# A hybrid attention and SSD decoder layer: norm blocks fetched up to four ahead and multiplied 26 steps later, one convolution at a time, second readers emitted later

## The chip, the cores and the metric

The kernel runs on one core of a Trainium2 chip. The metric is the device time of one execution in microseconds (us), and of several executions the median. Engines go by the profile's names: PE is TensorE (PEld its weight loads), DVE is VectorE, ACT is ScalarE, POOL is GpSimd, SP is SyncE, which issues the DMAs here; SPq is its queue of them.

## The reference

One decoder layer over 512 prompt tokens and 8 x 8 sampled tokens, 576 in all, with 2048 features:

```python
h = rmsnorm(x, norm_pre)
u = jnp.einsum('btd,de->bte', h, w_in)
q, k, v, g_a, z, xbc, dt = jnp.split(u, SPLIT_POINTS, axis=-1)
o_a = swa_prompt(q, k, v, attn_sink)
attn_out = rmsnorm(o_a * jax.nn.silu(g_a), attn_norm)
xbc_c = jax.nn.silu(causal_conv(xpad, conv_w, conv_b))
y, h_new = ssd(xs, dt, A, Bm, Cm, h0, chunk)
yz = (y + d_skip * xs) * jax.nn.silu(z)
ssm_out = rmsnorm(yz, ssm_norm)
mix = jnp.concatenate([attn_out, ssm_out], axis=-1)
out = jnp.einsum('bte,ed->btd', mix, w_out)
return x + rmsnorm(out, norm_post), new_k, new_v, new_conv, h_new
```

(Cut: shapes, masks and the sampled tokens' branch are left out.) `ssm_out` is normed in four groups of 512 features, `attn_out` over all 2048. The caches, the convolution's tails and the states are outputs too. All is fp32.

## The kernel before

*The matmuls.* Features lie on the 128 partitions, the 576 tokens along the free axis in two halves of 288. fp32 accuracy comes from three passes: weight tile and activation are each split into a rounded half and a rest, and `mm3` issues three matmuls of 128x128 by 128x288 (lines 348 to 350): high by high, high by rest, rest by high. A unit of weights, 128x512, is loaded into one of nine `raw` buffers (line 309), rounded into `w[:, 0]` by ACT (line 329), and its rest is taken by DVE (line 332) into `w[:, 1]`; there are four `w` buffers, so a unit is split up to three ahead. In most of the input product a unit serves eight calls of `mm3`. Column tiles come singly or, later, in pairs, which save one product in eight and need sums of weight units on POOL (line 269). The input product's columns come in the order of four head groups of the state part (B, C and four x tiles each, with the z gates between), then keys, values, queries and gates of attention; the output product runs in two passes, first over the state half of `mix`, then over the attention half.

*The order of work.* Nothing is scheduled by the compiler: instructions stand on each engine in the order in which the program emits them. The main program emits the matmuls and calls `sch.tick()` once before each `mm3`: a step. Everything else, some two dozen kinds of side task, is a Python generator on the class `Schedule`: it emits a few instructions and says by `yield n` that it goes on n steps later. `yield from wait(...)` asks again at each step. If the main program itself lacks a buffer it ticks on without a matmul, so that side work is emitted with no matmul between. An engine executes its instructions strictly in that order and stands where one has to wait; so do SP's transfers.

*The parts that the change touches.* `renorm` (line 1129) finishes the norm of a head group (four blocks of 128 features) or of attention (sixteen). The blocks lie in DRAM, in `m_d`; their factors, one a token, are stored to `r_d` (lines 838 and 839, in `finish`) and read back over all partitions by `factors` (line 845) 8 steps later. Then, 10 steps on, one block after the other: load (line 1135), 8 steps, multiply by the factors and gamma on DVE (line 1137), a step, store to `m_d` (line 1139), a step. 32 blocks in all.

`conv_task` (line 1157) takes one 128-feature tile of B, C or x: first tap on ACT (line 1163), three taps on DVE (line 1166), tanh on ACT (line 1168), gate on DVE (lines 1171, 1175). It holds two of four `scratch` buffers, U and y; the main program takes one for each new tile (line 1190). The first two tiles, B and C of group 0, have been kept raw and start together (`conv_raw`). There are 24 tiles, and a single column tile takes 32 steps.

`qb_task` (line 937) is one pair of attention heads and 256 queries: scores, softmax, transposes into the bank `pt` (line 1003), copies of `pt` to `pT[1]` by ACT (line 1010) and, masked, to `pT[0]` by DVE (line 1012 or 1014), 9 steps, value matmuls (line 1024). `sample` (line 1338) updates the sampled tokens' states: a matmul into the bank `pS` (line 1382), 2 steps, an addition on DVE (line 1385). `dt_task` (line 728) is a chain of some 20 small DVE instructions (lines 747 to 770) on the step sizes, once, early on.

Of the kernel before, what the change touches and what calls it, by code (L numbers as in the profile page):

```python
# [172 lines left out]
def wait(cond):  # L173
    while not cond():
        yield 1
# [3 lines left out]
def kern(ctx: ExitStack, tc: tile.TileContext, a: dict, o: dict):  # L179
    nc = tc.nc  # L180
    V, S, G, PE = nc.vector, nc.scalar, nc.gpsimd, nc.tensor
    dma = nc.sync.dma_start
# [17 lines left out]
    sch = Schedule()  # L200
# [7 lines left out]
    slots = Slots(sch, [f"S{i}" for i in range(NBIG)], make)  # L208
# [40 lines left out]
    m_d = [dr.tile([P, T], F32, name=f"m_d{j}", tag=f"m_d{j}") for j in range(32)]  # L249
# [592 lines left out]
    def factors(k):  # L842

        t = yield from slots.get()
        dma(t[:, :T], bass.AP(tensor=r_d.tensor, offset=r_d.offset + k * T, ap=[[0, P], [1, T]]))
        return t
# [90 lines left out]
    def qb_task(st, jj, m, u):  # L937
# [70 lines left out]
        pT4 = [t[:, :512].rearrange("p (f q k) -> p f q k", f=2, q=2) for t in pT]  # L1008

        S.copy(pT[1][:, :512], pt)  # L1010
        if f:
            V.tensor_tensor(pT4[0][:, :, 1], ptv[:, :, 1], stri.unsqueeze(1).broadcast_to([P, 2, P]), ALU.mult)
        else:
            V.tensor_tensor(pT[0][:, :512].rearrange("p (e k) -> p e k", e=4), pt.rearrange("p (e k) -> p e k", e=4),
                            stri.unsqueeze(1).broadcast_to([P, 4, P]), ALU.mult)
        banks.put(pt)
        yield 9
        for q in range(2):
            qb = 2 * m + q
            w0 = 0 if qb else 1  # L1020
# [108 lines left out]
    def renorm(k0, row, gamma):  # L1129

        Rt = yield from factors(row)
        yield 10
        for k in k0:
            t = yield from slots.get()
            dma(t, m_d[k])
            yield 8
            V.scalar_tensor_tensor(t, t, gamma[:, k % 16:k % 16 + 1], Rt, op0=ALU.mult, op1=ALU.mult)
            yield 1
            dma(m_d[k], t)
            yield 1  # L1140
            slots.put(t)
            ready["m", k] = True
        slots.put(Rt)
# [6 lines left out]
    class Group:  # L1150
        def __init__(self, g):
# [2 lines left out]
            self.done = set()  # L1154
            self.M, self.mid = {}, 0

    def conv_task(grp, name, box, k):
        U = box[0]
        Us = U[:, 515:603].rearrange("p (b w) -> p b w", w=11)
        G.tensor_copy(tails[:, k, 0], U[:, 512:515])  # L1160
        G.tensor_copy(tails[:, k, 1:9], Us[:, :, 8:11])
        y = yield from scratch.get()
        S.activation(y[:, :600], U[:, 0:600], AF.Identity, scale=cw[:, k, 0:1], bias=cw[:, k, 4:5])  # L1163
        yield 3
        for w in range(1, 4):
            V.scalar_tensor_tensor(y[:, :600], U[:, w:w + 600], cw[:, k, w:w + 1], y[:, :600], op0=ALU.mult, op1=ALU.add)  # L1166
            yield 2
        S.activation(U[:, :600], y[:, :600], AF.Tanh)
        yield 3
        dst = yield from slots.get()  # L1170
        V.scalar_tensor_tensor(dst[:, :TP], U[:, :TP], 1.0, y[:, :TP], op0=ALU.add, op1=ALU.mult)

        def smp(t):
            return t[:, 515:603].rearrange("p (b w) -> p b w", w=11)[:, :, 0:8]
        V.scalar_tensor_tensor(dst[:, TP:T].rearrange("p (b w) -> p b w", w=8), smp(U), 1.0, smp(y), op0=ALU.add, op1=ALU.mult)
        scratch.put(U, y)
        if name[0] == "C":
            if grp.g > 1:
                yield from wait(lambda: len(groups[grp.g - 2].done) == 5)
            G.tensor_copy(Cs[grp.g % 2][:, 0:TS], dst[:, TP:T])  # L1180
        yield 2
        grp.bc[name[0] if name[0] != "x" else name[2]] = dst
# [155 lines left out]
    def sample(grp, n, cs, C, Bt, xes, sms, E):  # L1338
# [34 lines left out]
        def seq(b, h0):  # L1373
            w = b // 4
            yield from wait(lambda: b < 2 or b - 2 in issued)
            Bs = BR[:, 2 * P + P * (b % 2):3 * P + P * (b % 2)]
            S.activation(Bs[:96], Bw[w][:96].bitcast(F32), AF.Copy, scale=bsel4[:96, b % 4:b % 4 + 1])
            hv = h0[:, :512].rearrange("p (h d) -> p h d", h=8)
            G.tensor_tensor(hv, hv, dch[:, 4 + b, h8].unsqueeze(2).broadcast_to([P, 8, 64]), ALU.mult)  # L1379
            yield 13  # L1380
            pS = yield from banks.get()
            PE.matmul(pS, Bs[:96], Xs[w][:96], start=True, stop=True)
            issued.add(b)
            yield 2
            V.tensor_tensor(h0[:, :512], h0[:, :512], pS, ALU.add)
            banks.put(pS)
            yield 2
            dma(o["ss"][g, :, b], h0[:, :512])
            smalls.put(h0)
            fin.append(b)  # L1390
# [70 lines left out]
    for entry[0] in range(len(PROGRAM)):  # L1461
# [17 lines left out]
        else:  # L1479
            f, t = conv_block(groups[g], name)  # L1480
# [44 lines left out]
    def attn_end():  # L1525
        yield from wait(lambda: attn_done[0] == 18)
        yield from sumA.finish(4 * D, 0)
        yield 8
        yield from renorm(range(16), 0, gam[0])
# [279 lines left out]
```

## Time and profile before

| | |
|---|---|
| median of 3 runs | 1655.22 us (1653.7 to 1661.37) |
| the profiled execution: its own time, and its span | 1653.8 us, 1652.0 us |
| granted TensorE clock, mean over the span | 0.981 |
| busy PE, DVE, ACT, POOL | 1598.8, 1095.8, 771.1, 389.4 us |
| moved by DMA | 222.98 MB, 135 GB/s over the span |

The span is the profiler's, from the first to the last instruction; the time has 1.8 us more around it. Busy time of PE counts a matmul from its start to its modelled end, and matmuls overlap, so holes are seen as missing busy time in short stretches, not as a share of the whole. A wait is put down to the instruction that stands first on its engine; all behind it waits with it.

### The profile page before, as it was taken

How to read it: one execution, taken by the hardware profiler on the slowest of the kernel's cores; microseconds unless marked ns; L12 is line 12 of the kernel's file. 1: busy time of each engine (PE TensorE's matmuls, PEld its weight loads, DVE VectorE, ACT ScalarE, POOL GpSimd, SP SyncE). 2: the span in 40 equal slices, each digit the busy share in tenths (PEclk: the TensorE clock that was granted, in tenths of full speed). 3: DMA queues.
4: the chain of work that ended last, by engine and by line, in shares of the span. 5: the costliest groups of instructions: out<-in, count | busy, mean ns of one | idle time of the engine just before them, and what ended most of it. 6: DMA issues, size and time to landing. Idle time of an engine off the chain costs nothing.

```text
span 1652.0 us, 31869 instructions
## 1 busy us (share of the span) xinstructions
PE 1598.8 (97%) x12158; PEld 1542.6 (93%) x12158; DVE 1095.8 (66%) x2185; ACT 771.1 (47%) x1849; POOL 389.4 (24%) x420
## 2 busy tenths in 40 slices
PE   8999999999999999999999999999999999999995
PEld 8899999999989998998999999999899999999995
DVE  7656755775667567476778868777686455655556
ACT  6433433444434445364655636656573322544440
POOL 3201222221312220342223213222111211023323
PEclk9999999999999999999999999999999999999997
DMA  6324356546565648446314322323461356723235
GB/s 238 89 74 110 90 180 187 146 163 188 142 154 160 186 131 279 132 134 135 103 58 126 87 75 75 97 71 109 132 201 46 96 153 216 271 86 103 91 100 186
DMA packets 157977, 222.98 MB, mean 135 GB/s; under 512 B 32160, under 2 KB 66080, under 8 KB 157792
## 3 DMA queue, kind: packets, MB, share of 16 engines
q1 hardware_dynamic: 157824, 220.95, 44.5%
q8 instruction: 95, 1.56, 0.4%
q14 instruction: 58, 0.48, 0.1%
HBM read 182.26 MB, written 40.60 MB: 135 GB/s over the span
## 4 chain that ended last, share of the span: by engine, by line
PE 80%; DVE 8%; DMA 6%; ACT 2%; issue 2%; SPq 1%; POOL 0%; DVEq 0%; ACTq 0%; POOLq 0%
PE bank L348 23%; PE bank L350 23%; PE bank L349 22%; DMA s<-m_d 4%; PE bank L1024 2%; DVE w L332 1%; DMA r_d<-t 1%; DVE u L1166 1%; PE bank L1286 1%; PE bank L1003 1%; DMA s<-z_d 1%; PE bank L954 1%; PE bank L955 1%; PE bank L1298 1%; DVE s L1667 1%
## 5 line engine op out<-in xcount | busy, mean ns | idle before, releaser
L348 PE MATMUL bank<-x,w 128*128 128x288 f32 x3288 | 999.9, 304 | 6.4 <-DVE eT L420 2.6
L350 PE MATMUL bank<-x,w 128*128 128x288 f32 x3288 | 983.4, 299 | 17.2 <-DVE w L332 17.2
L349 PE MATMUL bank<-x,w 128*128 128x288 f32 x3288 | 980.6, 298 | 1.8 <-DVE x L542 1.8
L348 PEld LDWEIGHTS bank<-x,w 128*128 128x128 f32 x3288 | 625.7, 190 | 26.5 <-issue 15.1
L350 PEld LDWEIGHTS bank<-x,w 128*128 128x128 f32 x3288 | 626.8, 191 | 19.2 <-DVE w L332 19.2
L349 PEld LDWEIGHTS bank<-x,w 128*128 128x128 f32 x3288 | 625.8, 190 | 7.2 <-issue 3.8
L332 DVE TENSOR_TENSOR w<-raw,w 128x512 fp32r<-128x512 f32 x476 | 386.7, 818 | 130.4 <-ACT w L329 120.5
L329 ACT CAST w<-raw 128x512 fp32r<-128x512 f32 x476 | 289.4, 615 | 270.5 <-PE bank L349 226.0
L269 POOL TENSOR_TENSOR raw<-raw,raw 128x512 f32<-128x512 f32 x52 | 78.0, 1499 | 190.9 <-issue 163.3
L1166 DVE SCALAR_TENSOR_TENSOR u<-u,c_convwb,u 128x600 f32<-128x600 f32 x72 | 67.4, 940 | 24.0 <-ACT u L1163 22.9
L269 POOL TENSOR_TENSOR raw<-sum,raw 128x512 f32<-128x512 f32 x26 | 33.8, 1300 | 182.2 <-DVE w L332 171.2
L991 ACT ACTIVATE m<-m,t 128x128 f32<-128x128 f32 x128 | 49.9, 391 | 38.7 <-DVE t L986 38.7
L1236 ACT ACTIVATE m<-m,a_tok 128x128 f32<-128x128 f32 (+1 forms) x160 | 53.3, 381 | 19.3 <-DMA m<-aT_d 19.3
L998 ACT ACTIVATE m<-m,t 128x128 f32<-128x128 f32 x128 | 41.0, 392 | 45.5 <-DVE t L995 45.4
L542 DVE TENSOR_TENSOR x<-s,x 128x288 fp32r<-128x288 f32 x112 | 48.4, 479 | 18.9 <-ACT x L537 18.6
L830 POOL TENSOR_TENSOR s<-s,s 128x512 f32<-128x512 f32 (+2 forms) x42 | 46.0, 1096 | 56.2 <-ACT s L828 55.6
L1379 POOL TENSOR_TENSOR m<-m,dch 128x512 f32<-128x512 f32 x32 | 38.0, 1216 | 89.4 <-PE bank L1401 47.4
L1631 POOL TENSOR_TENSOR s<-s,s 128x288 f32<-128x288 f32 x28 | 23.0, 825 | 149.1 <-ACT s L1628 149.1
L269 POOL TENSOR_TENSOR sum<-raw,raw 128x512 f32<-128x512 f32 x26 | 35.5, 1366 | 94.1 <-DMA raw<-in_win_dram 56.1
L1272 POOL TENSOR_TENSOR m<-m,de 128x512 f32<-128x512 f32 (+1 forms) x20 | 25.3, 1264 | 112.9 <-DVE m L1265 96.7
L1163 ACT ACTIVATE u<-u,c_convwb 128x600 f32<-128x600 f32 x24 | 21.2, 889 | 65.5 <-DVE u L443 61.7
L1434 POOL TENSOR_TENSOR s<-s,s 128x576 f32<-128x576 f32 x16 | 24.8, 1552 | 98.2 <-DMA s<-z_d 88.2
(254 smaller groups left out, 1766.8 us busy)
## 6 DMA issues: line engine op xcount, KB each, us to landing
raw<-in_win_dram SPq DMA_DIRECT2D x304, 256.0 KB
raw<-in_wout_dram SPq DMA_DIRECT2D x128, 256.0 KB
s<-m_d SPq DMA_DIRECT2D x80, 288.0 KB
m_d<-s SPq DMA_DIRECT2D x48, 288.0 KB
s<-in_xT_dram SPq DMA_DIRECT2D x40, 288.0 KB
m<-aT_d SPq DMA_DIRECT2D x32, 256.0 KB
m<-in_h0T_dram SPq DMA_DIRECT2D x32, 256.0 KB
out_ss_dram<-m SPq DMA_DIRECT2D x32, 256.0 KB
```

Of the source, the lines that this page charges most:

```text
L269: G.tensor_tensor(dst, x, y, op)
L329: S.copy(w[:, 0], x)
L332: V.tensor_tensor(w[:, 1], x, w[:, 0].bitcast(F32), ALU.subtract)
L348: PE.matmul(out, w[:, 0, c], x[:, 0], start=start, stop=False, skip_group_check=True)
L349: PE.matmul(out, w[:, 0, c], x[:, 1], start=False, stop=False, skip_group_check=True)
L350: PE.matmul(out, w[:, 1, c], x[:, 0], start=False, stop=stop, skip_group_check=True)
L542: V.tensor_tensor(t[:, 1], src, t[:, 0].bitcast(F32), ALU.subtract)
L830: G.tensor_tensor(self.acc[:, c0:c0 + n], self.acc[:, c0:c0 + n], sq[:, :n], ALU.add)
L991: S.activation(p4[:, e], p4[:, e], AF.Exp, bias=nm[:, e:e + 1], scale=0.125, accum_out=den[:, e:e + 1])
L998: S.activation(p4[:, e], p4[:, e], AF.Copy, scale=den[:, e:e + 1])
L1166: V.scalar_tensor_tensor(y[:, :600], U[:, w:w + 600], cw[:, k, w:w + 1], y[:, :600], op0=ALU.mult, op1=ALU.add)
L1236: S.activation(Mv[q][:n, h, :n], Mv[q][:n, h, :n], AF.Relu, bias=a_tok[:n, c, k:k + 1], scale=-1.0)
```

## The change

Three edits, all in the order of emission. In `renorm` the loads are a task of their own, 8 steps apart, with up to four blocks loaded and not yet multiplied, as long as more than five buffers are free; a block is multiplied 26 steps after its load, and its store stands 3 steps behind. The load task starts 5 steps after the factors' reload (4, and one until it runs). In `conv_task` a flag lets one convolution's taps run at a time, and the waits between its instructions are longer. In `qb_task` DVE's copy of `pt` comes 4 steps after ACT's, and the value matmuls 8 after that; in `sample` the addition comes 5 steps after its matmul. No instruction that computes is added or taken away.

```diff
@@ -1008,13 +1008,14 @@
         pT4 = [t[:, :512].rearrange("p (f q k) -> p f q k", f=2, q=2) for t in pT]
 
         S.copy(pT[1][:, :512], pt)
+        yield 4
         if f:
             V.tensor_tensor(pT4[0][:, :, 1], ptv[:, :, 1], stri.unsqueeze(1).broadcast_to([P, 2, P]), ALU.mult)
         else:
             V.tensor_tensor(pT[0][:, :512].rearrange("p (e k) -> p e k", e=4), pt.rearrange("p (e k) -> p e k", e=4),
                             stri.unsqueeze(1).broadcast_to([P, 4, P]), ALU.mult)
         banks.put(pt)
-        yield 9
+        yield 8
         for q in range(2):
             qb = 2 * m + q
             w0 = 0 if qb else 1
@@ -1129,13 +1130,23 @@
     def renorm(k0, row, gamma):
 
         Rt = yield from factors(row)
-        yield 10
-        for k in k0:
-            t = yield from slots.get()
-            dma(t, m_d[k])
-            yield 8
+        ahead, k0 = [], list(k0)
+
+        def load():
+            for k in k0:
+                yield from wait(lambda: len(ahead) < 4 and len(slots.free) > 5)
+                t = yield from slots.get()
+                dma(t, m_d[k])
+                ahead.append((k, t, sch.t + 26))
+                yield 8
+
+        yield 4
+        sch.spawn(load())
+        for _ in k0:
+            yield from wait(lambda: ahead and ahead[0][2] <= sch.t)
+            k, t, _ = ahead.pop(0)
             V.scalar_tensor_tensor(t, t, gamma[:, k % 16:k % 16 + 1], Rt, op0=ALU.mult, op1=ALU.mult)
-            yield 1
+            yield 3
             dma(m_d[k], t)
             yield 1
             slots.put(t)
@@ -1154,19 +1165,24 @@
             self.done = set()
             self.M, self.mid = {}, 0
 
+    conv_busy = [False]
+
     def conv_task(grp, name, box, k):
         U = box[0]
         Us = U[:, 515:603].rearrange("p (b w) -> p b w", w=11)
         G.tensor_copy(tails[:, k, 0], U[:, 512:515])
         G.tensor_copy(tails[:, k, 1:9], Us[:, :, 8:11])
+        yield from wait(lambda: not conv_busy[0])
+        conv_busy[0] = True
         y = yield from scratch.get()
         S.activation(y[:, :600], U[:, 0:600], AF.Identity, scale=cw[:, k, 0:1], bias=cw[:, k, 4:5])
-        yield 3
+        yield 6
         for w in range(1, 4):
             V.scalar_tensor_tensor(y[:, :600], U[:, w:w + 600], cw[:, k, w:w + 1], y[:, :600], op0=ALU.mult, op1=ALU.add)
-            yield 2
+            yield 3
+        conv_busy[0] = False
         S.activation(U[:, :600], y[:, :600], AF.Tanh)
-        yield 3
+        yield 6
         dst = yield from slots.get()
         V.scalar_tensor_tensor(dst[:, :TP], U[:, :TP], 1.0, y[:, :TP], op0=ALU.add, op1=ALU.mult)
 
@@ -1381,7 +1397,7 @@
             pS = yield from banks.get()
             PE.matmul(pS, Bs[:96], Xs[w][:96], start=True, stop=True)
             issued.add(b)
-            yield 2
+            yield 5
             V.tensor_tensor(h0[:, :512], h0[:, :512], pS, ALU.add)
             banks.put(pS)
             yield 2
```

How the order changes, in three places. First DVE at the first convolutions: `u` are their buffers; line 1166 before, 1181 now, is a tap, 1171 and 1175, now 1187 and 1191, the gate; 443 evicts a matmul's bank, and 332 takes a weight unit's rest. Before:

```order
L1166 SCALAR_TENSOR_TENSOR u_846<-u_832,c_convwb,u_846 128x600
L1171 SCALAR_TENSOR_TENSOR s_861<-u_827,u_842 128x512
L1175 SCALAR_TENSOR_TENSOR s_861<-u_827,u_842 128x64
L1171 SCALAR_TENSOR_TENSOR s_864<-u_832,u_846 128x512
L1175 SCALAR_TENSOR_TENSOR s_864<-u_832,u_846 128x64
L443 TENSOR_TENSOR u_868<-bank_71,R 128x288
L443 TENSOR_TENSOR u_868<-bank_72,R 128x224
L443 TENSOR_TENSOR u_868<-bank_72,R 128x8x8
L1166 SCALAR_TENSOR_TENSOR u_876<-u_868,c_convwb,u_876 128x600 x3
L332 TENSOR_TENSOR w_98<-raw_91,w_98 128x512
```

Now:

```order
L1181 SCALAR_TENSOR_TENSOR u_842<-u_827,c_convwb,u_842 128x600
L332 TENSOR_TENSOR w_98<-raw_91,w_98 128x512
L1181 SCALAR_TENSOR_TENSOR u_842<-u_827,c_convwb,u_842 128x600 x2
L332 TENSOR_TENSOR w_95<-raw_92,w_95 128x512
L1187 SCALAR_TENSOR_TENSOR s_929<-u_827,u_842 128x512
L1191 SCALAR_TENSOR_TENSOR s_929<-u_827,u_842 128x64
L332 TENSOR_TENSOR w_96<-raw_93,w_96 128x512
L1181 SCALAR_TENSOR_TENSOR u_932<-u_832,c_convwb,u_932 128x600 x2
L332 TENSOR_TENSOR w_97<-raw_85,w_97 128x512
L443 TENSOR_TENSOR u_977<-bank_70,R 128x288
```

Before, six taps (the last is shown), the gates, three evictions and three further taps stood in one piece ahead of the next weight split. Now weight splits stand among the first tile's and the second's taps, and the third tile's follow later, among the dt chain (lines 747 to 770):

```order
L747 MEMSET s_1056 128x32
L749 TENSOR_TENSOR s_1056<-bank_68,s_689 128x128
L749 TENSOR_TENSOR s_1056<-bank_68,s_689 64x32
L752 SCALAR_TENSOR_TENSOR s_1056<-s_1056 128x160
L1181 SCALAR_TENSOR_TENSOR u_1021<-u_850,c_convwb,u_1021 128x600
L757 TENSOR_SCALAR s_1056<-s_1056 128x160
L758 RECIPROCAL s_1056<-s_1056 128x160
L759 TENSOR_TENSOR s_1056<-s_1056 128x160
L760 TENSOR_TENSOR s_1057<-s_1056 128x160
L761 TENSOR_SCALAR s_1057<-s_1057 128x160
L1181 SCALAR_TENSOR_TENSOR u_1021<-u_850,c_convwb,u_1021 128x600
L332 TENSOR_TENSOR w_96<-raw_88,w_96 128x512
```

Nine instructions of that chain and two taps stand here between one weight split and the next.

Then DVE in group 1, where a multiply (line 1137, now 1148) stands near the scan (lines 1318 to 1330, now 1334 to 1346). Before:

```order
L1166 SCALAR_TENSOR_TENSOR u_4928<-u_4920,c_convwb,u_4928 128x600
L1137 SCALAR_TENSOR_TENSOR s_4914<-s_4914,c_gssm,s_4879 128x576
L1318 TENSOR_TENSOR m_4730<-bank_68,m_4730 128x512
L1320 TENSOR_TENSOR m_4730<-m_4730,bank_71 128x512
L1330 SCALAR_TENSOR_TENSOR s_3542<-s_3542,c_dskip,m_4730 128x128
L1330 SCALAR_TENSOR_TENSOR s_3718<-s_3718,c_dskip,m_4730 128x128
L1330 SCALAR_TENSOR_TENSOR s_3892<-s_3892,c_dskip,m_4730 128x128
L1330 SCALAR_TENSOR_TENSOR s_4026<-s_4026,c_dskip,m_4730 128x128
L1166 SCALAR_TENSOR_TENSOR u_4928<-u_4920,c_convwb,u_4928 128x600
L332 TENSOR_TENSOR w_98<-raw_92,w_98 128x512
```

Now:

```order
L1334 TENSOR_TENSOR m_4801<-bank_67,m_4801 128x512
L1336 TENSOR_TENSOR m_4801<-m_4801,bank_68 128x512
L1346 SCALAR_TENSOR_TENSOR s_3566<-s_3566,c_dskip,m_4801 128x128
L1346 SCALAR_TENSOR_TENSOR s_3740<-s_3740,c_dskip,m_4801 128x128
L1346 SCALAR_TENSOR_TENSOR s_3919<-s_3919,c_dskip,m_4801 128x128
L1346 SCALAR_TENSOR_TENSOR s_4055<-s_4055,c_dskip,m_4801 128x128
L1148 SCALAR_TENSOR_TENSOR s_4906<-s_4906,c_gssm,s_4881 128x576
L332 TENSOR_TENSOR w_96<-raw_85,w_96 128x512
```

The multiply of block 20 now stands behind the scan's instructions and directly ahead of a weight split; before, it stood ahead of the scan, with the next weight split behind that.

Last SP in the norm of attention: line 1135, now 1139, loads a block, 1139, now 1150, stores it, 309 loads weights. Before:

```order
L1139 DMA m_d_108<-s_14882 128x576
L1135 DMA s_14923<-m_d_109 128x576
L309 DMA raw_93<-in_wout_dram 128x512
L309 DMA raw_85<-in_wout_dram 128x512
L1139 DMA m_d_109<-s_14923 128x576
L1135 DMA s_14964<-m_d_110 128x576
L1139 DMA m_d_110<-s_14964 128x576
```

Now:

```order
L1139 DMA s_14899<-m_d_111 128x576
L1150 DMA m_d_108<-s_14798 128x576
L309 DMA raw_93<-in_wout_dram 128x512
L309 DMA raw_85<-in_wout_dram 128x512
L1139 DMA s_14934<-m_d_112 128x576
L1150 DMA m_d_109<-s_14832 128x576
L1139 DMA s_14967<-m_d_113 128x576
L1150 DMA m_d_110<-s_14862 128x576
```

Before, a block's store stood directly ahead of the next block's load, and the load of block 10 (`m_d_110`) directly ahead of its own store. Now the loads of the three blocks after it stand between a block's load and its store.

## Rows read from the trace of the kernel before

**Rows 1.** The page: busy us (share of the span) xinstructions of each engine.
```profile
PE 1598.8 (97%) x12158; PEld 1542.6 (93%) x12158; DVE 1095.8 (66%) x2185; ACT 771.1 (47%) x1849; POOL 389.4 (24%) x420
```

**Rows 2.** Stretches: us, busy PE, PEld, DVE, ACT, POOL, clock, DMA share, GB/s.
```profile
60.00:85.00 25.00, 21.26 (x138) 20.43 (x137) 18.78 (x38) 9.77 (x15) 7.87 (x15) 0.86 0.20 55
85.00:110.00 25.00, 24.04 (x159) 22.61 (x158) 15.18 (x38) 6.80 (x13) 0.58 (x4) 0.86 0.36 91
...
460.00:480.00 20.00, 16.12 (x111) 15.88 (x110) 11.62 (x20) 6.02 (x15) 2.79 (x4) 0.91 0.70 187
630.00:650.00 20.00, 17.21 (x119) 16.75 (x119) 18.80 (x42) 12.92 (x32) 1.32 (x1) 0.83 0.82 263
755.00:775.00 20.00, 16.31 (x109) 15.62 (x109) 10.36 (x20) 8.75 (x26) 4.09 (x4) 0.83 0.66 210
800.00:1100.00 300.00, 299.79 (x2399) 288.81 (x2400) 232.38 (x492) 171.06 (x486) 79.98 (x73) 1.00 0.29 87
1215.00:1225.00 10.00, 8.15 (x65) 7.29 (x64) 7.04 (x20) 6.93 (x24) 0.00 (x0) 1.00 0.45 143
1335.00:1395.00 60.00, 54.78 (x384) 53.94 (x383) 33.37 (x50) 15.89 (x28) 12.11 (x8) 0.94 0.63 202
1400.00:1425.00 25.00, 25.00 (x190) 25.00 (x189) 16.59 (x35) 11.54 (x28) 0.00 (x0) 1.00 0.90 310
1450.00:1550.00 100.00, 100.00 (x753) 100.00 (x753) 55.48 (x86) 41.83 (x85) 32.30 (x30) 1.00 0.28 88
```

**Rows 3.** Waits, whole span: who waited for whom, total us, times, longest.
```profile
DVE s L1137 <- DMA s<-m_d: 71.4, 27, 7.5
...
DVE m L1014 <- ACT m L1010: 44.4, 15, 4.3
...
POOL sum L269 <- DMA raw<-in_wout_dram: 38.0, 8, 9.0
...
DVE m L1012 <- ACT m L1010: 28.0, 15, 2.2
...
PE bank L350 <- DVE w L332: 17.2, 8, 3.9
```

**Rows 4.** Timeline of SP from 450 us: start, us, line, operation, out<-in, count.
```profile
452.39 0.52 SPq L839 DMA_DIRECT2D r_d<-t  x1
...
461.68 0.33 SPq L845 DMA_DIRECT2D s<-r_d  x1
...
463.74 0.38 SPq L1135 DMA_DIRECT2D s<-m_d  x1
```

**Rows 5.** Timeline, 460 to 474 us; in brackets idle before and releaser.
```profile
468.16 0.82 DVE L1137 SCALAR_TENSOR_TENSOR s<-s,c_gssm,s 128x576 f32<-128x576 f32 x1 [7.44 <-DMA s<-m_d]
...
472.14 0.69 DVE L332 TENSOR_TENSOR w<-raw,w 128x512 fp32r<-128x512 f32 x1
...
472.88 0.41 PE L350 MATMUL bank<-x,w 128*128 128x288 f32 x1 [3.88 <-DVE w L332]
```

**Rows 6.** Timeline of SP from 744 us.
```profile
755.33 0.92 SPq L1135 DMA_DIRECT2D s<-m_d  x1
```

**Rows 7.** Timeline, 760 to 765 us, VectorE and TensorE.
```profile
761.18 0.82 DVE L1137 SCALAR_TENSOR_TENSOR s<-s,c_gssm,s 128x576 f32<-128x576 f32 x1 [7.51 <-DMA s<-m_d]
...
764.45 0.61 PE L350 MATMUL bank<-x,w 128*128 128x288 f32 x1 [3.69 <-DVE w L332]
```

**Rows 8.** Waits of the DMA queue on SP, whole span.
```profile
SPq L1139 <- DMA s<-m_d: 63.0, 27, 4.9
```

**Rows 9.** Timeline of VectorE, 60 to 76 us, around the first convolutions.
```profile
62.25 4.60 DVE L1166 SCALAR_TENSOR_TENSOR u<-u,c_convwb,u 128x600 f32<-128x600 f32 x6
...
74.15 0.68 DVE L332 TENSOR_TENSOR w<-raw,w 128x512 fp32r<-128x512 f32 x1
```

**Rows 10.** DMA, 1330 to 1400 us: packets, bytes, mean rate, packets by size.
```profile
DMA packets 7190, 14.15 MB, mean 202 GB/s; under 512 B 788, under 2 KB 788, under 8 KB 7185
```

**Rows 11.** Lines, VectorE, 80 to 95 us: count, busy us, mean ns, idle.
```profile
L764 DVE SCALAR_TENSOR_TENSOR s<-s 128x160 f32<-128x160 f32 x8 | 2.6, 322 | 0.2
```

## The prediction

> **What bounds the kernel now.** I read the page first. TensorE (PE) is busy 97% of the span and no other engine more than 66% [rows 1]. So the time is the chain of matmuls, and a change to VectorE (DVE), ScalarE and the DMA queue can only win what PE loses in holes. Next I read the stretches: in 1450 to 1550 us PE never idles, the granted clock is full and 753 matmuls take 100 us, 0.133 us each [rows 2]. One step of the schedule is three of them, so **a step is worth 0.40 us**. A hole is a stretch in which busy PE is shorter than the stretch, or the clock is under 1.00; the second costs (1 - clock) x length, as the lower level (1.2 GHz) is half the upper one (2.4 GHz).
>
> Then I read the waits, to see who makes the holes. PE's longest is for the second half of a split weight tile, DVE line 332: 17.2 us in 8 pieces. In the same answer DVE waited 71.4 us, in 27 of 32 cases, at line 1137 for `s<-m_d`: the norm multiply stands on DVE before its block has landed, and all of DVE, the weight splits too, stands behind it [rows 3]. One such place end to end: the block's load is issued at 463.74 [rows 4], the multiply starts at 468.16 after 7.44 us of wait, it and seven more instructions take 4.0 us until a weight split starts at 472.14, and PE resumes at 472.88 after 3.88 us of nothing [rows 5]. The same two head groups later: 7.51 us on DVE, 3.69 on PE [rows 7]. So **DVE runs some 3.6 us ahead of PE**, and only what a wait takes beyond that becomes a hole.
>
> **The change part by part.**
>
> *Norm blocks.* Before, a multiply was emitted 8 steps after its load, 8 x 0.40 = 3.2 us; the loads took 468.16 - 463.74 = 4.4 and 761.18 - 755.33 = 5.9 us from issue to multiply [rows 4 to 7]. Now it is 26 steps, 10.4 us. For the later blocks of a run that covers both by over 4 us. The first block of a run needs a second look, since its load stands behind something: the per-token factors are stored to `r_d`, and their reload (line 845) holds SP until that store has landed, 461.68 - 452.39 = 9.3 us [rows 4]; everything behind it on SP waits too. Counted from that store, the first multiply was emitted 8 + 10 + 8 = 26 steps later and is now 8 + 5 + 26 = 39 (the spawned load runs in the next step). That is 13 steps, 5.2 us, so the waits of 7.4 and 7.5 us should fall to 2.2 and 2.3, under DVE's lead of 3.6. The load itself moves up, 13 steps behind the store where it was 18, still behind line 845. Nothing is added: 32 loads, multiplies and stores as before.
>
> What it is worth, by idle PE plus clock, where this wait stands in front of the hole [rows 2]: 460 to 480: 3.9 + 0.09 x 20 = 5.7 us; 630 to 650: 2.8 + 0.17 x 20 = 6.2; 755 to 775: 3.7 + 3.4 = 7.1; 1335 to 1395, three holes: 5.2 + 0.06 x 60 = 8.8. Sum 27.8. At 630 to 650 DVE is busy 18.8 of 20 us, so part of that hole is plain load and not the wait: I take **26**.
>
> SP gains too: it stood 63.0 us behind stores that waited for the same blocks [rows 8]; the store now comes 3 steps (1.2 us) behind its multiply, which takes 0.82 [rows 5]. I count nothing, for weight loads were not what PE waited for.
>
> *One convolution at a time.* At the start two convolutions run together, and the main program, wanting a third buffer, lets 12 steps of side work be emitted with no matmul between. On DVE that is six taps, four gate instructions, three evictions and three more taps, 62.25 to 74.15, before the next weight split [rows 9]. PE has its hole there: in 60 to 85, 3.7 us idle and 0.14 x 25 = 3.5 of clock, 7.2 [rows 2]. In the new order three weight splits stand among the same instructions. Against it: the work is not gone but later, and now meets the dt chain. Between its splits into w_95 and w_97 the new order has some 20 instructions of the dt chain, three taps and a gate, some 10 us of DVE (0.77 a tap [rows 9], 0.32 one of the chain's [rows 11]) where PE needs two units of eight steps, 6.4 us, and a few small matmuls. The excess is about DVE's lead, so I charge 3 for a shorter hole there: net **4**. Later blocks come one per 32 steps and need some 24, so they stay as they were but for the spacing of the taps.
>
> *Second reader of a bank later.* DVE waited 28.0 + 44.4 us for ScalarE's copy of the same bank (lines 1012, 1014) [rows 3]; in four steps, 1.6 us, other DVE work can go first. But from 800 to 1100 us PE loses 0.2 us in all, at the full clock [rows 2], so this wait is hidden by DVE's lead. The value matmuls come 3 steps later, which helps the one place where PE waited for that copy, 1215 to 1225, 1.9 us idle [rows 2]: **1**. Were DVE's lead gone, 1.9 would be the loss in place of a gain. The same edit in the state update hides likewise: nothing.
>
> *Everything else* shifts by up to 13 steps, and chance meetings of side tasks move. The hole at 85 to 110 (1.0 + 3.5 us [rows 2]) and those at either end have other causes and stay. I charge **3** for new meetings, two thirds of that one hole.
>
> Sum: 26 + 4 + 1 - 3 = **28 us**. The profiled execution took 1653.8 (span 1652.0); the median of the three runs is 1655.2, 1.4 above. I predict 1655 - 28 = **1627**. Bounds: with every term full and no new hole 27.8 + 7.2 + 1.9 = 37, and 4.5 more if the hole at 85 to 110 goes too: 1614. With half the norm term, no convolution gain and 3 of new holes, 11: 1644.
>
> *A rule weighed.* A 288 KB block took 4.4 and 5.9 us to land, at DMA shares of 0.70 and 0.66 [rows 2, 4 to 7]. The Trainium skill (DMA: Bandwidth & Descriptors, Latency and other measured facts) gives HBM's access latency as 0.2 us on average and 2 us at high load, which speaks against loading further ahead, since transfers get denser. By it the first multiplies would wait up to an estimated 1.8 us more, 4.1 where I have 2.3, past DVE's lead in the head groups, and the gain would be some 4 us less: 1631. No row here has a norm wait at the new density, so the trace bears out neither.
>
> **The rivals.** (1) *Half of it.* The factors' reload stays on SP, and DVE is full in 630 to 650: the first multiply of a run still eats DVE's lead, now where the scan's work stands. Then the holes of 5.7, 6.2 and 7.1 stay at half, and the dt hole replaces the one removed: 28 - 9.5 - 4 = 15, 1640. For it: a margin of 1.3 us is thin. Against: the later multiplies hardly wait. That the change does not do what it says ends here too: a load waits for more than five free buffers, and were there fewer, blocks would again come one at a time.
> (2) *No change.* PE's holes only move: the time freed lets DVE and ScalarE run into other bunches (the dt chain, the scans) that cost as much. It needs 20 us or more of new holes, where the holes that the norm did not make, 60 to 110 and 1215 to 1225, are 14 [rows 2]. 1651.
> (3) *Slower*: **weights late.** Norm loads and stores come on the one SP queue at one per 8 steps where there was one per 10 and its waits. From 1330 to 1400 the core moves 14.15 MB at 202 GB/s [rows 10], the DMA engines 0.63 busy [rows 2]; the same bytes in 16 x 8 + 18 = 146 steps, 58 us, would be 244 GB/s and a share of 0.76. GpSimd's sums have waited 38.0 us for output weights, 9.0 at the longest [rows 3]. If weights then land late, each of some 22 loads in that stretch can hold PE; to end over 8 us slower it takes 36 us, 1.6 a load: 1664. Against: from 1400 to 1425 the core moves 310 GB/s at 0.90 and PE is busy 25.00 of 25.00 [rows 2].
>
> **How the numbers follow.** My case has 0.68 and spans 1614 to 1637; rival 1 0.18, 1635 to 1647; rival 2 0.09; rival 3 0.05. 1627 is the first case's. The range, 1613 to 1643, leaves out the last two and the edges of the others. About 0.5% (8 us) is what a measurement here can tell from no change: faster 0.87, same 0.08, slower 0.05.
>
> **What would show it.** Right: the multiply's wait for `s<-m_d` under 15 us in total, PE's wait for line 332 under 6, the clock full from 450 to 780 and from 1330 to 1400, SP no longer behind norm stores, no hole near 70 us and perhaps a smaller one near 85 to 100. Wrong: holes at the same six places with another name on DVE, or PE and the sums waiting for `raw`. If the six close and the time still stands, the stretches will show where it went.

## The result and the profile after

The changed kernel takes **1616.1 us** (median of 4 runs, 1613.6 to 1619.5), the kernel before 1654.7 beside it: a ratio of 0.976 (95% interval 0.974 to 0.979), 38.6 us less. Forecast were 1627 us and a gain of 28. The profiled execution took 1619.5 us (span 1617.7), 3.4 above its median, so the two traces differ by 34.3 us of span.

First the page of the kernel after, busy us of each engine, against [rows 1]:

```profile
PE 1581.9 (98%) x12158; PEld 1526.8 (94%) x12158; DVE 1095.8 (68%) x2185; ACT 768.1 (47%) x1849; POOL 383.9 (24%) x420
```

Every engine executes as many instructions as before. The mean granted clock went from 0.981 to 0.993: (1 - 0.981) x 1652 = 31.4 us were lost to the lower level before, (1 - 0.993) x 1618 = 11.3 are now. So 20 of the 34 us came back as clock and the other 14 as idle time closed. In most stretches of [rows 2] that lost time, idle time and the lower clock stand together.

The stretches of the kernel after (us, busy PE, PEld, DVE, ACT, POOL, clock, DMA share, GB/s), against [rows 2]:

```profile
60.00:85.00 25.00, 25.00 (x188) 24.75 (x189) 19.77 (x40) 10.00 (x16) 6.92 (x13) 1.00 0.30 91
85.00:110.00 25.00, 25.00 (x179) 23.83 (x179) 16.68 (x39) 11.16 (x24) 2.28 (x6) 0.93 0.41 99
...
460.00:480.00 20.00, 20.00 (x155) 18.89 (x154) 17.59 (x33) 10.05 (x25) 5.50 (x13) 1.00 0.52 159
600.00:655.00 55.00, 48.02 (x362) 44.25 (x362) 40.32 (x78) 30.22 (x70) 8.37 (x6) 1.00 0.74 235
630.00:650.00 20.00, 17.24 (x137) 15.53 (x135) 16.28 (x35) 14.58 (x33) 2.88 (x3) 1.00 0.67 220
755.00:775.00 20.00, 20.00 (x161) 19.65 (x160) 18.27 (x34) 10.99 (x37) 6.21 (x5) 1.00 0.43 139
...
1335.00:1395.00 60.00, 60.00 (x452) 60.00 (x451) 36.17 (x67) 24.20 (x53) 3.04 (x2) 1.00 0.75 246
```

PE has no hole left at 70, 460, 760 and 1335 to 1395. It still has at 600 to 655, 7 us, which is the largest loss in the middle of the run. As the program runs up to 34 us earlier now, a fixed stretch holds slightly other work than it held before; the table further down avoids that.

The waits, engines first, then those of SP's queue, against [rows 3, 8]:

```profile
POOL sum L269 <- DMA raw<-in_wout_dram: 37.5, 7, 10.5
...
PE bank L350 <- DVE w L332: 3.2, 4, 1.5
...
DVE s L1148 <- DMA s<-m_d: 0.8, 2, 0.6
...
DVE m L1013 <- ACT m L1010: 0.3, 1, 0.3
```

```profile
SPq L845 <- DMA r_d<-t: 40.4, 5, 9.0
SPq L1150 <- DVE s L1148: 36.7, 23, 3.5
```

The multiply's wait fell from 71.4 us to 0.8, PE's for line 332 from 17.2 to 3.2, DVE's for ScalarE's copy (line 1013 now) from 72.4 to 0.3. SP still stands behind norm stores, 36.7 us of it, and now waits for the multiply alone; before, it waited 63.0 us for the block [rows 8] and 26.6 more for the multiply:

```profile
SPq L1139 <- DVE s L1137: 26.6, 29, 2.3
```

And it stands 40.4 us at line 845, behind stores of factors (34.5 before). That row matters below.

### The profile page after: what moved, and what is told of

Same layout as the page of the kernel before. It is cut to its first block, busy times and chain, and to the rows that moved or that the text cites. A ratio compares the mean times of both kernels' runs of the same rounds, so it can differ in the third digit from the quotient of the medians.

```text
span 1617.7 us, 31918 instructions
## 1 busy us (share of the span) xinstructions
PE 1581.9 (98%) x12158; PEld 1526.8 (94%) x12158; DVE 1095.8 (68%) x2185; ACT 768.1 (47%) x1849; POOL 383.9 (24%) x420
## 4 chain that ended last, share of the span: by engine, by line
PE 86%; DVE 4%; DMA 4%; ACT 3%; issue 1%; SPq 1%; POOL 1%; DVEq 0%; ACTq 0%; POOLq 0%
PE bank L348 25%; PE bank L350 24%; PE bank L349 24%; PE bank L1025 2%; DMA s<-z_d 1%; PE bank L1302 1%; PE bank L955 1%; PE bank L954 1%; PE bank L1003 1%; DVE s L1683 1%; PE bank L1314 1%; DVE w L332 1%; DMA r_d<-t 1%; PE bank L1312 1%; POOL s L1450 1%
## 5 line engine op out<-in xcount | busy, mean ns | idle before, releaser
L348 PEld LDWEIGHTS bank<-x,w 128*128 128x128 f32 x3288 | 619.1, 188 | 21.9 <-issue 16.3
L349 PEld LDWEIGHTS bank<-x,w 128*128 128x128 f32 x3288 | 619.3, 188 | 7.1 <-issue 3.8
L350 PEld LDWEIGHTS bank<-x,w 128*128 128x128 f32 x3288 | 619.9, 189 | 4.1 <-DVE w L332 4.1
L1181 DVE SCALAR_TENSOR_TENSOR u<-u,c_convwb,u 128x600 f32<-128x600 f32 x72 | 63.9, 887 | 14.3 <-ACT u L1178 13.7
L542 DVE TENSOR_TENSOR x<-s,x 128x288 fp32r<-128x288 f32 x112 | 50.5, 501 | 15.6 <-ACT x L537 15.5
L828 ACT ACTIVATE s<-s 128x512 f32<-128x512 f32 (+1 forms) x27 | 17.7, 655 | 77.0 <-DVE s L1035 42.5
L269 POOL TENSOR_TENSOR sum<-raw,raw 128x512 f32<-128x512 f32 x26 | 34.2, 1314 | 74.4 <-DMA raw<-in_wout_dram 37.5
```

Source lines behind the costliest of these rows:

```text
L269: G.tensor_tensor(dst, x, y, op)
L348: PE.matmul(out, w[:, 0, c], x[:, 0], start=start, stop=False, skip_group_check=True)
L349: PE.matmul(out, w[:, 0, c], x[:, 1], start=False, stop=False, skip_group_check=True)
L350: PE.matmul(out, w[:, 1, c], x[:, 0], start=False, stop=stop, skip_group_check=True)
L542: V.tensor_tensor(t[:, 1], src, t[:, 0].bitcast(F32), ALU.subtract)
```

## The same matmul in both traces

Both kernels issue the same 9864 matmuls of lines 348 to 350 in the same order. The start of the n-th in the trace before, less its start in another trace, is what has been gained up to there. The table gives the gain within each stretch (times of the kernel before; n = 300, 600, 1500, 3600, 4200, 4800, 7800, 8400; a few tenths are noise). N is the norm edit, C the convolution edit, R the two reader edits; "forecast" is the prediction's terms put into these stretches, its charge of 3 us for new meetings left out, as are the 1.8 us that it took off the hole at 630 to 650.

| stretch, us | forecast | change | N alone | C alone | R alone | C+R | N+R | N+C |
|---|---|---|---|---|---|---|---|---|
| 62 to 122, convolutions, dt | 4 | 9.6 | -1.1 | 11.1 | -0.3 | 9.6 | -0.5 | 9.5 |
| 263 to 608, scans | 5.7 | 12.6 | 3.9 | 5.7 | 1.3 | 9.9 | 9.4 | 8.5 |
| 608 to 704 | 6.2 | **-6.5** | 5.6 | 0.5 | -1.4 | -9.6 | 2.6 | 2.3 |
| 704 to 810 | 7.1 | 7.1 | 6.6 | 3.5 | -1.0 | 0.8 | 7.0 | 8.3 |
| 810 to 1317, attention | 1 | 3.2 | -0.1 | -0.9 | 3.0 | 3.3 | 2.6 | -0.3 |
| 1317 to 1408, attention norm | 8.8 | 9.1 | 9.2 | -1.2 | 0.3 | -2.3 | 9.2 | 9.1 |
| up to the end | 28 | 34.3 | 23.3 | 18.2 | 1.2 | 10.9 | 30.0 | 36.7 |

Every trace here is one execution, set against the one trace of before (1653.8 us). Beside the experiments the kernel before took 1660 us; so their ratios show some 5 to 7 us more gain than these traces, and differences of 5 us between kernels timed apart are not told from none. The change itself was timed beside 1654.7, so its ratio is not on the same footing as theirs.

## The experiments

**One edit alone, and two of three.** Six kernels, each the kernel before with whole edits of the change.

```diff
 e1: renorm as changed
 e2: conv_task as changed
 e3: qb_task and sample as changed
 e4: the change, renorm as before
 e5: the change, conv_task as before
 e6: the change, qb_task and sample as before
```

e1, norm alone:

> The kernel before with the new norm task alone (loads ahead, multiply 26 steps later). Theory A (each edit closes its own holes, and they add): the wait for s<-m_d falls under 3 us, the holes at 468, 635, 760, 1339, 1354 and 1382 us close, 27 us gained: 1627, between 1624 and 1631; the hole at 70 to 75 us stays. Theory B (the edits share VectorE's lead; the norm's gain needs the others' freed time): holes reopen beside the old places, under 20 us gained: 1635 or more.

e2, convolution alone:

> The kernel before with the new convolution task alone. Theory A: the hole at 70 to 75 us and its clock dip close, and the stretch 85 to 110 loses less; 7 to 10 us gained: 1645 to 1648; the six norm holes stay as they are, 27 us. Theory B: the taps' spacing also takes load from VectorE beside the scans, so the norm holes at 468 and 635 shrink too and more than 12 us are gained: under 1643.

e3, readers alone:

> The kernel before with the two later second readers alone. VectorE's waits for ScalarE's copy of the transposed bank fall from 72 to under 5 us. Theory A: hidden by VectorE's lead, 0 to 3 us gained: 1652 to 1655. Theory B: VectorE's lead is what closes holes elsewhere (1193 to 1222 us, the state updates), 5 us or more gained: under 1650.

e4, without the norm edit:

> The changed kernel with the norm task of before. Theory A: the six norm holes are back, 27 us slower than the change: 1641 to 1646. Theory B: the other two edits give VectorE more lead, so the norm's waits are covered better and the loss is under 20 us: under 1636.

e5, without the convolution edit:

> The changed kernel with the convolution task of before. Theory A (the edits close separate holes): the hole at 70 to 75 us and its dips are back, 8 to 10 us slower than the change, about the norm alone: ratio to before 0.981 to 0.983. Theory B (the edits close the same holes, since a wait on VectorE costs TensorE only where a weight split stands soon behind it, and every edit moves that): the convolution is worth as much as when alone, 15 us or more: ratio 0.986 or more.

e6, without the reader edits:

> The changed kernel without the two later second readers. Theory A: they are hidden, 0 to 4 us slower than the change: ratio 0.976 to 0.979. Theory B: they cost rather than gain beside the new convolutions, as convolution with readers (e4) was 6 us slower than convolution alone (e2): faster than the change by 3 us or more, ratio under 0.9745.

| edits | median, us | ratio to before, 95% | wait for `s<-m_d` | PE's for line 332 |
|---|---|---|---|---|
| N | 1629.8 | 0.982 (0.980 to 0.983) | 2.1 | 2.4 |
| C | 1637.5 | 0.986 (0.985 to 0.988) | 60.4 | 6.1 |
| R | 1653.6 | 0.997 (0.995 to 0.998) | 68.7 | 14.4 |
| C+R | 1643.3 | 0.990 (0.988 to 0.991) | 77.5 | 14.5 |
| N+R | 1623.8 | 0.978 (0.976 to 0.980) | 0.7 | 2.5 |
| N+C | 1617.3 | 0.974 (0.972 to 0.976) | 0.5 | 0.2 |
| N+C+R, the change | 1616.1 | 0.976 (0.974 to 0.979) | 0.8 | 3.2 |

Against the expectations: e1, e3 and e4 came out at theory A's times, e2 and e6 at theory B's. For e6 that is weak, as its interval overlaps that of the change. e5 fits neither: taking the convolution out of the change costs only 4.3 us by the traces. It loses the 10.1 at the start and wins 9.2 back from 608 to 704.

By the traces the three give 23.3 + 18.2 + 1.2 = 42.7 us alone and 34.3 together. (The ratios give 59 and 39, but were not taken beside the same time of the kernel before.) They overlap, and the table of stretches shows where. The start is the convolution's: 9.5 to 11.1 us wherever that edit is, nothing without. The attention norm is the norm's: 9.1 or 9.2 with it, a loss or 0.3 without. The attention stretch is the reader's: about 3 with it, nothing without. DVE's waits for ScalarE's copy are nearly all hidden, as argued: N+C keeps 73.4 us of them and is as fast as the change. Between 263 and 810 each edit shifts the others' work, and there the gains don't add.

The convolution alone was the surprise: the wait for `s<-m_d` stays at 60.4 us, yet PE's wait for line 332 is down to a third. Its waits, and a piece of DVE's timeline (start, us, engine, line, operation, count, idle before):

```profile
DVE s L1137 <- DMA s<-m_d: 60.4, 23, 5.8
...
PE bank L350 <- DVE w L332: 6.1, 5, 1.9
```

```profile
454.34 0.82 DVE L1137 SCALAR_TENSOR_TENSOR s<-s,c_gssm,s 128x576 f32<-128x576 f32 x1 [5.68 <-DMA s<-m_d]
...
457.91 0.68 DVE L332 TENSOR_TENSOR w<-raw,w 128x512 fp32r<-128x512 f32 x1
...
461.01 0.81 DVE L1137 SCALAR_TENSOR_TENSOR s<-s,c_gssm,s 128x576 f32<-128x576 f32 x1
```

With the order shifted, a later multiply stands behind a scan's instructions (line 1335, up to 461) and finds its block there. A wait costs by what stands behind it, and an edit elsewhere changes what does. The other side is C+R: 77.5 us of the same wait, 12.7 at the longest, and 9.6 us lost between 608 and 704.

**Is it the distance to the multiply, or the loads ahead?** The change with 8 steps in place of 26:

```diff
-                ahead.append((k, t, sch.t + 26))
+                ahead.append((k, t, sch.t + 8))
```

> The changed kernel with one number put back: a norm block is multiplied 8 steps after its load, as before, while up to four blocks are still fetched ahead. Theory A (the distance in the order from load to multiply is what closes the norm holes): the multiply stands in front of work while its block is still under way, its wait for the block is back at 40 us or more in total, PE waits for line 332 over 8 us, and the ratio to the kernel before lies at 0.985 to 0.992, near the 0.990 of the change without its norm edit. Theory B (fetching several blocks at once is enough, since all but the first then have landed early): wait under 15 us, ratio at or under 0.980.

1649.5 us, ratio 0.993 (0.992 to 0.994). It is the distance: with up to four blocks under way as in the change, the wait is back at 54.2 us in 18 cases, with 14.2 more at one multiply that the profile puts down to another load, and PE's for line 332 is at 15.3.

```profile
DVE s L1148 <- DMA s<-m_d: 54.2, 18, 10.3
...
DVE s L1148 <- DMA s<-in_xT_dram: 14.2, 1, 14.2
```

The gain is even smaller than theory A gave. A reason that fits, but was not tried alone: the first multiply of a run is now emitted 13 steps after the factors' reload, where before it was 18. The timeline of one such place, SP, then DVE, then PE:

```profile
753.37 0.33 SPq L845 DMA_DIRECT2D s<-r_d  x1
753.75 0.93 SPq L1139 DMA_DIRECT2D s<-m_d  x2
```

```profile
759.46 1.71 DVE L1148 SCALAR_TENSOR_TENSOR s<-s,c_gssm,s 128x576 f32<-128x576 f32 x1 [10.35 <-DMA s<-m_d]
```

```profile
762.29 0.58 PE L348 MATMUL bank<-x,w 128*128 128x288 f32 x1 [6.98 <-DVE t L994]
```

The block is issued right behind the reload and multiplied 5.7 us later, as in [rows 6, 7]; but DVE had stood there 10.35 us, and PE stood 6.98. By the count of the table this kernel has the convolution's 9.5 us from 62 to 122 and loses 11.6 from 608 to 704.

**Only the first block later.** The kernel before, with the first load 13 steps later:

```diff
-        yield 10
+        yield 23
```

> The kernel before, its norm task starting 13 steps later and else unchanged: one block at a time, multiplied 8 steps after its load. Theory A (a wait costs only beyond VectorE's lead of 3.6 us): the first multiplies wait 1 to 3 us, the holes at 468, 760 and 1339 close, those at 1354 and 1382 stay, total wait for s<-m_d 45 to 60 us, 10 to 17 us gained, ratio 0.990 to 0.994. Theory B (the waits themselves are the cost, so the loads have to be ahead): under 6 us gained, ratio over 0.996.

1655.9 us, ratio 0.998 (0.996 to 0.999): theory B's number. The holes at 460 and 755 did close, as theory A had it (19.56 and 19.26 of 20 us, clock 1.00). But those in the norm of attention stayed (0.5 us gained from 1317 to 1408 by the count of the table), the wait fell only to 54.1, as 24 multiplies still wait, and a new hole of 5.8 us came at 653, a loss of 5.6 from 608 to 704. SP, then ACT, then PE:

```profile
643.26 0.33 SPq L1139 DMA_DIRECT2D m_d<-s  x1
...
645.55 6.16 SPq L1347 DMA_DIRECT2D m<-in_h0T_dram  x8
652.29 0.33 SPq L1139 DMA_DIRECT2D m_d<-s  x1
```

```profile
657.76 0.76 ACT L537 CAST x<-s 128x288 fp32r<-128x288 f32 x2 [14.45 <-DMA m_d<-s]
```

```profile
659.09 0.61 PE L348 MATMUL bank<-x,w 128*128 128x288 f32 x1 [5.80 <-ACT w L329]
```

A norm store got behind eight loads of states on SP, was issued 9 us after the one ahead of it, and ACT stood 14.45 us, by the profile's releaser for such a store to let a buffer go; a weight's first half (line 329) stood behind ACT.

**The flag or the spacing.** The convolution edit in two halves, each on the kernel before:

```diff
 e8: only the flag
+        yield from wait(lambda: not conv_busy[0])
+        conv_busy[0] = True
...
+        conv_busy[0] = False
 e10: only the spacing
-        yield 3
+        yield 6
...
-            yield 2
+            yield 3
...
-        yield 3
+        yield 6
```

> The kernel before with one convolution at a time, its instructions spaced as before. Theory A: the flag removes the 12 steps without a matmul, so the hole at 70 to 75 us closes and 7 to 10 us are gained, ratio 0.994 to 0.996, and the spacing gave the rest of the 22.7 us of the convolution alone (e2), in the norm holes at 468, 635 and 760. Theory B: the flag gives all, 18 us or more, ratio under 0.989.

> The kernel before with the new spacing of the convolution's steps alone (6, 3, 6 in place of 3, 2, 3) and no flag, so that two convolutions may still run together at the start. Theory B of the convolution (the spacing shifts the norm multiplies behind other VectorE work, and that gave some 18 of the 23 us of the convolution edit): ratio 0.987 to 0.991, PE waits for line 332 under 10 us, the hole at 70 to 75 us stays. Theory A (the flag and the spacing only work together, the new order as such closes nothing): ratio 0.996 to 1.0, PE waits for line 332 14 us or more.

The flag gives 0.997 (0.996 to 0.999), the spacing 0.994 (0.993 to 0.996), both 0.986. Neither run fits a theory: the flag closed the first hole, as its theory A had it, but gained less than was priced for it; the spacing lies between its two. By the traces they give 2.9 and 2.1 us alone, 18.2 together. At the start the flag alone gains 5.4 us and the spacing alone loses 0.8, together they gain 11.1. Without the flag PE meets the next hole in the dt chain, and without the spacing a smaller one. PE's timeline of e8, then of e10, where before it stood 0.96 us:

```profile
93.86 0.41 PE L779 MATMUL bank<-s,c_tri 128*128 128x32 f32 x2 [2.53 <-DVE s L770]
```

```profile
88.44 0.41 PE L779 MATMUL bank<-s,c_tri 128*128 128x32 f32 x2 [4.74 <-DVE s L770]
```

The rest of the spacing's gain is 4.7 us in the scans (263 to 608), which the flag alone has not (0.4).

**The reader edit in the state update.** The change with that one wait as before, the attention's reader still later; and the same with the first combination of token blocks started 80 steps later, as a version that might beat both:

```diff
-            yield 5
+            yield 2
 e12, also:
-            sch.spawn(combine(x_block))
+            sch.spawn(combine(x_block), 80)
```

> The change without the later second reader in the state update (2 steps as before), the attention's second reader still moved. Theory A (the reader edits add nothing once the norm and the convolution are changed, and only reshuffle chance meetings of side tasks): ratio 0.973 to 0.977, the same as the change within its interval, but a changed set of holes between 600 and 660 us. Theory B (the state update's edit costs the holes at 604 to 655 us, 6.5 us of the change's loss): ratio 0.971 to 0.973 and PE busy over 50 of 55 us from 600 to 655.

> A version that may beat both kernels: the change without the state update's edit, and with the first combination of the token blocks started 80 steps later, away from the start of its stage. If the holes after the scans, near 1165 to 1205 us, are a meeting of that side task with weight splits, they go and the ratio is 0.968 to 0.972. If they have another cause, the ratio is that of the kernel without the state update's edit within 0.002, or higher where the later task meets another bunch.

1614.3 us, ratio 0.972 (0.970 to 0.974), with 53.7 of 55 us: theory B's numbers. And 1616.6 us, 0.973 (0.971 to 0.975): the later combination brings nothing, and PE's idle time from 1165 to 1196 us stays, 3.5 and 3.4 us. Without the state update's edit the trace ends 7 us before the change's (41.4 us gained, not 34.3). Some 1 of these lies ahead of the first state update, at 224 us, and cannot be the edit's; 9.2 lie in one stretch, 608 to 704: 2.7 gained instead of 6.5 lost. The loss takes the convolution edit too, as N+R gains 2.6 there. The medians, 1614.3 and 1616.1, are only 1.8 apart and were not taken beside each other; the change's profiled execution was the slowest of its four. So what the edit costs in the median stays open. The stretch itself in e11 (columns as above):

```profile
600.00:655.00 55.00, 53.73 (x412) 50.77 (x411) 42.84 (x85) 34.67 (x77) 6.67 (x5) 1.00 0.79 254
```

The two timelines show what sits there. The change, SP, then ACT, then PE:

```profile
590.40 0.51 SPq L839 DMA_DIRECT2D r_d<-t  x1
...
600.68 0.33 SPq L845 DMA_DIRECT2D s<-r_d  x1
601.10 0.93 SPq L1241 DMA_DIRECT2D m<-aT_d  x2
```

```profile
606.65 0.40 ACT L1252 ACTIVATE m<-m,a_tok 128x128 f32<-128x128 f32 x1 [7.68 <-DMA m<-aT_d]
606.96 0.60 ACT L329 CAST w<-raw 128x512 fp32r<-128x512 f32 x1
```

```profile
607.61 0.40 PE L348 MATMUL bank<-x,w 128*128 128x288 f32 x1 [0.82 <-ACT w L329]
...
620.37 0.30 PE L1272 MATMUL bank<-ident,s 128*64 128x128 f32 x1 [2.27 <-DVE s L443]
...
644.07 0.40 PE L350 MATMUL bank<-x,w 128*128 128x288 f32 x1 [1.48 <-DVE w L332]
```

And e11, SP, then ACT:

```profile
586.03 0.51 SPq L839 DMA_DIRECT2D r_d<-t  x1
586.63 1.09 SPq L1241 DMA_DIRECT2D m<-aT_d  x2
...
596.92 0.37 SPq L845 DMA_DIRECT2D s<-r_d  x1
```

```profile
599.54 0.70 ACT L1252 ACTIVATE m<-m,a_tok 128x128 f32<-128x128 f32 x2 [11.92 <-DMA m<-aT_d]
```

The reload of the factors holds SP for some 10 us in both. In e11 the scan's loads (line 1241) were emitted ahead of it; in the change they stand behind it, go out at 601.10, and ACT waits 7.68 us for them with a weight split behind. The wait of e11 is longer, 11.92 us, and costs PE nothing: from 586 to 602 us PE is busy all 16 us. In the change PE stands 0.82 us for that weight; 2.27 us of idle follow at 620 (for an eviction at line 443), 1.48 at 644 and 1.29 at 650, both for line 332, in the middle of the next state update. So the loss begins with an order on SP that the edit shifted, and none of PE's 7.0 us of idle there is put down to a second reader. That the later holes follow from the first was not traced, and that the reload alone makes the loss was not tried.

## Why the prediction was right, and where it was off

The direction and its cause held, and 1616 lies within 1613 to 1643, but near the end of the range: 38.6 us came where 28 were forecast. By steps:

- **Norm blocks: right, and rightly sized.** Forecast 26 us. By the traces it gives 23.3 us alone, and taken out of the change it costs 23.4. Three stretches: 7.1 forecast and 6.6 to 8.3 measured at 704 to 810 with the edit, 8.8 and 9.1 at the attention norm, 6.2 and 5.6 (alone) at 608 to 704. The fourth, 263 to 608, came short alone, 3.9 of 5.7. Where I took the first block's wait to fall to 2.2 us, it went: the first multiply of the run at 446 us started at 457.0, 19.9 us after the factors' store at 437.1. I had priced its 39 steps at 0.40 us, 15.6; but 40 matmuls of line 348 start in the 20 us from 437 on, so a step takes 0.50 there, since the scans' matmuls stand between (158 matmuls in all, PE busy 20.00 of 20.00).
- **One convolution at a time: right place, mis-sized, 4 against 9.6.** The 7.2 at 60 to 85 us came in full. What failed is the charge of 3 for the dt chain, "The excess is about DVE's lead". The splits there end at 80.0, 85.8 and 91.9 us and PE comes to their units at 88.8, 96.2 and 103.2 (unit n's first use counted as 8 matmuls of line 350 a unit): a lead of 9 to 11 us, where I had taken the 3.6 of the norm holes for the whole run. And there was no excess: between the first and the last of these splits DVE took 11.9 us, but PE took 14.4 for the two units, not 6.4 and a little, since 54 small matmuls of the chain stand among them. The rest of the 5.6 is the old hole at 85 to 110, which I left standing: 4.5 us of idle and clock before, 1.8 now. DVE's rows, then the stretch of PE's two units:

```profile
79.30 0.68 DVE L332 TENSOR_TENSOR w<-raw,w 128x512 fp32r<-128x512 f32 x1
...
85.08 0.69 DVE L332 TENSOR_TENSOR w<-raw,w 128x512 fp32r<-128x512 f32 x1
...
91.16 0.69 DVE L332 TENSOR_TENSOR w<-raw,w 128x512 fp32r<-128x512 f32 x1
```

```profile
88.80:103.20 14.40, 14.40 (x104) 13.23 (x103) 10.77 (x24) 4.24 (x9) 2.28 (x6) 0.93 0.42 95
```

- **Second readers: 1 against 3 in attention.** DVE's 72 us of waits went. At the place that the prediction named, 1215 to 1225 us, the count gives 1.1, as forecast. The other 3.1 (0.9 was lost ahead of it) came at a place that it did not name. There PE stood 2.13 and 1.75 us for the split of `x` (lines 537 and 542) and the clock was 0.79 from 1190 to 1206; now it stands 1.65 us for the later second reader itself and 1.17 for `x`, at the full clock. So this part of the gain comes from a shifted order, not from the wait that was removed. PE before, then now:

```profile
1195.55 0.40 PE L348 MATMUL bank<-x,w 128*128 128x288 f32 x1 [2.13 <-ACT x L537]
1197.71 0.61 PE L349 MATMUL bank<-x,w 128*128 128x288 f32 x1 [1.75 <-DVE x L542]
...
1222.07 1.12 PE L1024 MATMUL bank<-m,m 128*64 128x128 f32 x12 [1.83 <-ACT m L1010]
```

```profile
1172.89 1.09 PE L1025 MATMUL bank<-m,m 128*64 128x128 f32 x16 [1.65 <-DVE m L1015]
...
1175.48 0.40 PE L349 MATMUL bank<-x,w 128*128 128x288 f32 x1 [1.17 <-DVE x L542]
```

  "The same edit in the state update hides likewise: nothing" failed in the traces, where it costs some 6 us through the order of other tasks.
- **New meetings: the sum about right by luck, made of two larger ones.** I charged 3, and 1.8 at 630 to 650. Between 608 and 704 us the change lost 6.5 where 6.2 were to be won, 12.7 off; in the scans ahead of it the shifted order gained 12.6 where 5.7 were due, 6.9 more. Net 5.8 against 4.8. What the forecast lacked is then the convolution's 5.6 and the attention readers' 2.2; the other 4 of the 38.6 us lie between the profiled executions and the medians.
- **The rivals.** Rival 3's traffic came as worked out: from 1335 to 1395 us a share of 0.75 and 246 GB/s, forecast 0.76 and 244; PE is busy 60.00 of 60.00, and the sums' wait for output weights is 37.5 us as before. So denser transfers cost PE nothing in that stretch. Rival 2, holes that only move, came in part: 600 to 655 us has 7.0 us of idle, 2.8 before, where it needed 20. Rival 1's point, a first multiply that still waits on the run's reload, is what e9 shows: true at 8 steps, gone at 26.
- **The rule weighed.** By the Trainium skill (DMA: Bandwidth & Descriptors, Latency and other measured facts) denser traffic could have added an estimated 1.8 us to the first waits. The change itself can't show it, as its multiplies stand far behind the loads: all norm waits together are 0.8 us, in 2 of 32, so the 4 us less of gain did not come. But e9 shows that blocks do land later. Its attention norm runs at 254 GB/s, where before it was 202 [rows 10]. From the run's second block on, a multiply that waited for its block started 4.7 us after the load's issue (median of 10), where before it was 3.0 (median of 14). The stretch of e9, then one multiply before (load issued at 1370.47) and one of e9 (issued at 1368.29):

```profile
1330.00:1385.00 55.00, 51.13 (x380) 50.48 (x380) 34.53 (x51) 15.66 (x27) 11.51 (x8) 1.00 0.78 254
```

```profile
1373.49 0.82 DVE L1137 SCALAR_TENSOR_TENSOR s<-s,c_ganorm,s 128x576 f32<-128x576 f32 x1 [2.82 <-DMA s<-m_d]
```

```profile
1373.17 0.82 DVE L1148 SCALAR_TENSOR_TENSOR s<-s,c_ganorm,s 128x576 f32<-128x576 f32 x1 [4.30 <-DMA s<-m_d]
```

  Whether a longer latency makes these 1.7 us or the loads that now stand closer together on one queue is not told apart. In the head groups the traffic did not get denser: e9's block at 753.75 was issued at 265 GB/s and took 5.7 us, that of [rows 6, 7] at 260 and took 5.9.
- **The signs named ahead.** Multiply's wait under 15: 0.8. Line 332 under 6: 3.2. Clock full from 450 to 780 and 1330 to 1400: yes. No hole at 70: yes; a smaller one at 85 to 100 did not come, PE is busy 25.00 of 25.00 at a clock of 0.93. SP no longer behind norm stores: no, 36.7 us of 89.6 stay; no hole of PE is put down to it.

## What to carry to other kernels

Where instructions run in the order of emission, don't price a wait by its length: price it by what stands behind it on its engine and by how far that engine is ahead at that very place, read split by split, not from one hole. Emit a consumer later by what its load really takes, counted from when the queue can issue it; fetching ahead without moving the consumer gave nothing that can be told (0.993 with it, 0.990 without the norm edit). And try edits of such an order one by one: by the traces, three that shift the same engines' order gave 34 us together and 43 as a sum of singles, and the state update's half of the readers cost some of what the others had won.

## What was not expected of the hardware

- The loads of a scan that were issued right behind the factors' store landed late: 586.63 to 599.54, 12.9 us until ACT could start on them, against 5.5 (601.10 to 606.65) for those issued after that store had landed. The store itself held the reload 10.3 and 10.9 us (590.40 to 600.68, 586.03 to 596.92). It is not a lack of bandwidth: in e11 the DMA engines were busy 0.06 of that time and moved 11 GB/s. What the loads behind the store waited for is not shown.

```profile
586.00:597.00 11.00, 11.00 (x90) 10.19 (x89) 4.68 (x11) 0.62 (x1) 2.05 (x2) 1.00 0.06 11
```

- The holes left in the change between 600 and 655 us, up to 2.27 us, brought no fall of the granted clock (1.00 in the stretch). Before, a hole of 3.69 us went with 0.83 over 20 us [rows 2, 7], but holes of 1.85 and 1.82, at 1356 and 1384 us, went with 0.89 over 15 us and 0.88 over 14. So the length of a single hole does not tell whether the clock falls.
